# Hybrid decoder layer: accumulators cleared in a step ahead of their rows, and a norm's squares ahead of the last convolution block

## The chip, the cores and the metric

One core of a Trainium2 chip runs the whole program in one launch. The metric is the device time of that launch in microseconds (us). The kernel before took 1226.35 us, the median of three runs (1225.25 to 1227.09).

## What is computed

One layer of a decoder over 256 tokens with a model width of 2048, in float32. The reference, cut to its frame:

```python
c_act = jax.nn.silu(c)
mod = (c_act @ w_mod[l] + b_mod[l])[:, None, :]             # w_mod: 2048 x 12288
sh_m, sc_m, g_m, sh_f, sc_f, g_f = jnp.split(mod, 6, axis=-1)
h = rmsnorm(x, mix_pre_w[l]) * (1 + sc_m) + sh_m
y = hybrid_mixer(h, ...)      # h @ w_in, short gated convolution | gated linear attention, then @ w_out
x = x + g_m * rmsnorm(y, mix_post_w[l])
h = rmsnorm(x, ffn_pre_w[l]) * (1 + sc_f) + sh_f
y = conv_ffn(h, ...)          # h @ w_up, causal convolution, silu gate, @ w_down
x = x + g_f * rmsnorm(y, ffn_post_w[l])
```

Inside the mixer the attention's output goes through a norm of its own, per head: `o = rmsnorm(o, gla_norm_w) * silu(r)`, and the two halves (convolution, attention) are concatenated ahead of `w_out`. The six vectors of `mod` are matrix-vector products: each is a sum of 2048 rows of `w_mod`, scaled by `c_act`.

## The kernel before

**Units.** Every large product is cut into units. A unit has one weight tile `raw`, loaded by SP; ScalarE (ACT) casts it to a short high part `wh` (L140), VectorE (DVE) forms the rest, `wl = raw - wh` (L145), and TensorE (PE) multiplies high by high, high by low and low by high. The ring of `raw` tiles has six places, those of `wh` and `wl` three each. I number the units in program order: u0 to u57 are the product with `w_in` (its last chunk of five row blocks is u40 to u57), u58 to u73 the product with `w_out`, u74 and on those with `w_up` and then `w_down`. The code's list `tail` begins at u40, so `tail[j]` is u(40+j). L579 to L581 are the three products of a `w_in` unit, L846 to L848 those of a `w_out` unit, L990 and L992 those of `w_up`.

**Order.** `drive` (L74) writes the program unit by unit: for unit i it runs the list `early`, then the load of unit i+2 and its cast (`prep`), then `wl` of unit i+1 (`low`), then `pre`, the products of unit i, `mid`, the evacuations that are due, and `late`. Everything that is not a unit's own work hangs in these four lists. Each engine runs its instructions strictly in the order that this writes; there is no scheduler behind it. So a DVE instruction that waits holds up every later one on DVE, the next `wl` among them, and PE waits for that `wl`.

**Modulation rows.** `mod_steps` (L160) computes a part of `mod` on DVE. One step loads a block of `w_mod` (SP, L184 or L187) and adds it, scaled by one column of `c_act`, to an accumulator (L136, a scalar_tensor_tensor). Sixteen steps, "rows" from here on, make a set. The accumulator is a tile `macc` of two buffers (or, for the small first set, a tile `big`); step 0 has POOL clear it (L178) and load the bias `b_mod` into its row 0 (L179), and then does the first row. `spread` (L68) puts the steps of a set evenly into the lists `early` and `mid` of a range of units. The sets in order are those of the chunks 1 to 3 of `w_in` (u0 to u9, u12 to u21, u22 to u31, with `lag` 1: a row is added one step behind its load), then `gacc` (`g_m`, u32 to u47), f1 (`sh_f` and `sc_f`, first half, u48 to u67 without u55 to u57), f2 and the last one in the `w_up` units; those four have `lag` 0.

**Other work in u40 to u57.** The levels of the attention (L704, L740, L761 on DVE, scores by PE at L678), its output and its norm: `norms` in the list `late` of u55 has ACT take eight sums of squares (L387) and one square root (L792), `scaled` in `pre` of u56 has DVE take the reciprocal (L797) and ACT scale eight blocks (L802), which PE then transposes (L810). The convolution runs in four pairs (`CONV`): `first` (c0) multiplies two blocks on DVE (L605, `cc = cc * cx`) and scales them on ACT (L607); c1 and c2 follow a unit later (L136 with `conv` scalars, L614, L616, L620). Partial sums of `cc`, `cx` and `v` in the last chunk are added to what stands in SBUF by an accumulating DMA: ACT copies the sum out of PSUM to `hf` (L459), POOL issues the DMA (L460).

Of the kernel before, what the change touches and what calls it, by code (L numbers as in the profile page):

```python
# [6 lines left out]
F32 = mybir.dt.float32  # L7
# [7 lines left out]
P = 128  # L15
D = 2048
T = 256
KT = D // P
# [23 lines left out]
MODS = (10, 22, 32, 48, 68)  # L42
CHUNK1 = 12
# [21 lines left out]
        self.hold = 0  # L65


def spread(steps, units):  # L68

    places = [p for u in units for p in (u.early, u.mid)]  # L70
    for i, f in enumerate(steps):
        places[i * len(places) // len(steps)].append(f)

# [30 lines left out]
def layer_kernel(ctx: ExitStack, tc, x, c, w_mod, b_mod, mix_pre_w, mix_post_w, w_in, conv_w, gate_w2, gate_b,  # L104
                 gla_norm_w, w_out, ffn_pre_w, ffn_post_w, w_up, ffn_conv_w, w_down, ident_in, masks_in, out):
    nc = tc.nc
# [6 lines left out]
    wts = ctx.enter_context(tc.tile_pool(name="wts", bufs=2))  # L113
# [5 lines left out]
    def nm(s):  # L119
        uid[0] += 1  # L120
        return f"{s}_{uid[0]}"

    def slot(shape, dt=F32):
        return big.tile(shape, dt, tag="big", name=nm("big"))
# [7 lines left out]
    def raw_tile(shape):  # L132
        return wts.tile(shape, F32, tag="raw", name=nm("raw"), bufs=NRAW)

    def stt(o, a, s, b, op0=ALU.mult, op1=ALU.add):
        nc.vector.scalar_tensor_tensor(o, a, s, b, op0=op0, op1=op1)  # L136
# [22 lines left out]
    b_mod_v = b_mod.rearrange("l (s n) -> l s n", s=6)  # L159

    def mod_steps(s0, n, a, w, nj, lag=0):

        accs, cur, rows = [], {}, []

        def use(j, r):
            stt(cur["acc"], r, c_act[:, j:j + 1], cur["acc"])

        def step(j):  # L170
            if j >= KT:
                use(*rows.pop(0))
                return
            if j == 0:
                acc = cur["acc"] = (slot([P, n, w]) if n * w <= 1024 else
                                    wts.tile([P, n, w], F32, tag="macc", name=nm("macc"), bufs=2))
                accs.extend(acc[:, s, :] for s in range(n))
                nc.gpsimd.memset(acc, 0.0)  # L178
                nc.gpsimd.dma_start(acc[0:1, :, :], b_mod_v[:, s0:s0 + n, a:a + w])  # L179
            m = nj if j < KT - nj or nj < 4 else 2  # L180
            if j % m == 0:
                cur["r"] = raw_tile([P, m, n, w])
                if m == 1:
                    nc.sync.dma_start(cur["r"][:, 0, :, :], w_mod_v[:, j, s0:s0 + n, a:a + w])  # L184
                else:
                    for s in range(n):
                        nc.sync.dma_start(cur["r"][:, :, s, :], w_mod_v[:, j:j + m, s0 + s, a:a + w])  # L187
            rows.append((j, cur["r"][:, j % m, :, :]))
            if j >= lag:
                use(*rows.pop(0))  # L190

        return accs, [lambda j=j: step(j) for j in range(KT + lag)]

    W0 = CHUNKS[0] * P
    first_acc = slot([P, 2, W0])
# [104 lines left out]
    def mod_columns(accs, n, pre, tagname):  # L300

        ash = const.tile([P, 2 * n], F32, tag=tagname, name=nm("ash"))
        st = {}

        def products(tiles=None):
            r = ones if len(accs) == 2 else ones_r
            if "ps" not in st:
                st["ps"] = bank([P, 4 * n + P])  # L310
            for o in (range(2 * n) if tiles is None else tiles):
                cs = slice((o % n) * P, (o % n + 1) * P)
                terms = (accs[o // n],) if len(accs) == 2 else accs[2 + o // n]
                for j, t in enumerate(terms):
                    nc.tensor.matmul(st["ps"][:, 2 * o:2 * o + P], t[:, cs], r, start=j == 0, stop=j == len(terms) - 1)  # L315

        def columns():
            nc.vector.tensor_copy(ash[:, :n], st["ps"][:, 0:2 * n:2])
            stt(ash[:, n:], st["ps"][:, 2 * n:4 * n:2], 1.0, pre, ALU.add, ALU.mult)

        return ash, products, columns

    def mod_rows(accs, post, tiles):

        parts = []

        def load():
            parts.extend(tiles())
            for h, g in enumerate(parts):
                nc.gpsimd.dma_start(g, post[:, h * 1024:(h + 1) * 1024].rearrange("a n -> (a n)")  # L330
                                    .partition_broadcast(P))

        sums = {}

        def products(h):
            terms, r = (accs[1], ones_r) if len(accs) == 2 else ((accs[0],), ones)
            for q in range(2):
                cs = slice(h * 1024 + q * 512, h * 1024 + (q + 1) * 512)
                ps = sums[h, q] = bank([P, 512])
                for j, term in enumerate(terms):  # L340
                    nc.tensor.matmul(ps, r, term[:, cs], start=j == 0, stop=j == len(terms) - 1)

        def used(h):
            for q in range(2):
                s = slice(q * 512, (q + 1) * 512)
                nc.vector.tensor_mul(parts[h][:, s], sums[h, q], parts[h][:, s])
            gpw[h] = parts[h]

        return load, products, used
# [114 lines left out]
    def modulate_chunk(ci, ash, early=None):  # L464

        k0, k1 = bounds[ci], bounds[ci + 1]
        kept = []

        def at_once():

            n = CHUNKS[0]
            for kts in pairs(k0, k1):
                ps, hf = early.pop(0), hf0[:, kts[0]:kts[-1] + 1, :]
                d = hts[kts[0] // 2] = slot([P, 2, 2, T], F32R)
                ab = [(ash[:, n + k:n + k + 1], ash[:, k:k + 1]) for k in kts]
                for i, (a, b) in enumerate(ab):
                    nc.scalar.activation(d[:, i, 0, :], ps[:, i, :], AF.Identity, bias=b, scale=a)
                for i, (a, b) in enumerate(ab):
                    nc.vector.tensor_scalar(hf[:, i, :], ps[:, i, :], a, b, op0=ALU.mult, op1=ALU.add)
                    h32.setdefault(ci, {})[kts[i]] = hf[:, i, :]  # L480
                act_low(d, hf)
                kept.append((kts, hf, None))

        def first():
            if early:
                at_once()
                return
            for kts in pairs(k0, k1):
                ps = turn_norm(xs, kts)
                hf = hf_tile()  # L490
                modulate(ps, kts, ash, CHUNKS[ci], k0, hf)
                for i, k in enumerate(kts):
                    h32.setdefault(ci, {})[k] = hf[:, i, :]
                kept.append((kts, hf, act_high(kts, hf, hts)))

        def second():
            for kts, hf, parts in kept:
                if parts:
                    act_low(*parts)
                for i, k in enumerate(kts):  # L500
                    gate_terms.append((k, hf[:, i, :]))

        return first, second
# [599 lines left out]
    chunks = [in_units(ci) for ci in range(len(CHUNKS))]  # L1103
# [53 lines left out]
    allin = [u for c in chunks for u in c] + owait  # L1157
# [3 lines left out]
    at, seconds = 0, []  # L1161
    for ci in range(1, len(CHUNKS)):
        n, us = CHUNKS[ci], chunks[ci - 1]
        st = {}
        st["accs"], steps = mod_steps(0, 2, bounds[ci] * P, n * P, 2 if n <= 4 else 1, 1)
        spread(steps, allin[CHUNK1 if ci == 2 else at:MODS[ci - 1]])
        at = MODS[ci - 1]

        def cols(ci=ci, n=n, st=st):
            st["ash"], products, st["columns"] = mod_columns(st["accs"], n, pre_c[:, bounds[ci]:bounds[ci + 1]], f"ash{ci}")  # L1170
            products()

        def mod0(ci=ci, st=st):
            st["columns"]()
            st["m"] = modulate_chunk(ci, st["ash"])
            st["m"][0]()

        us[-LEAD].early.append(cols)
        us[-LEAD].late.append(mod0)
        seconds.append((us[-LEAD + 1].late, lambda st=st: st["m"][1]()))  # L1180
        seconds.append((us[-LEAD + 1].late if ci > 1 else chunks[1][GATE1].mid, gate_products))
        seconds.append((chunks[ci][0 if ci > 1 else GATE1 + 1].mid, gate_sum))

    tail = chunks[-1] + owait
    gacc, gsteps = mod_steps(2, 1, 0, 2048, 1)
    spread(gsteps, [u for i, u in enumerate(allin) if at <= i < MODS[3]])
    load, ones_rows, rows_used = mod_rows(gacc, mix_post_w, lambda: [slot([P, 1024]) for _ in range(2)])
    r0 = 2
    owait[r0].late.append(load)
# [44 lines left out]
        tail[GATE[e] - 1].late.append(lambda e=e: turn(e))  # L1234
    for i, u in enumerate(CONV):
        c0, c1, c2 = conv_pair(i)
        tail[u].late.insert(0, c0)
        tail[u + 1].pre.append(c1)
        tail[u + (1 if i < 3 else 2)].late.append(c2)
    owait[8].late.append(warm_sqrt)  # L1240
# [238 lines left out]
```

## Time and profile before

| | before |
|---|---|
| median of three runs | 1226.35 us (1225.25 to 1227.09) |
| the profiled execution | 1225.3 us |
| its span, from the first to the last instruction | 1223.5 us |
| granted TensorE clock, mean | 0.992 |
| PE, DVE, ACT, POOL busy | 97%, 77%, 47%, 4% of the span |
| instructions | 17251 |

The profile is of one execution, so a time in it is to be set against 1225.3 us and not against the median. A row of the timeline has the start in us from the first instruction, the duration, the engine, the line, the operation with its output and inputs, a count of like instructions in one row (`x8`), and in brackets how long the engine sat idle before it and what released it. "PEclk" is the TensorE clock that was granted, as a share of full speed; PE's busy time also counts products at a reduced clock. DMA share is the mean busy share of the 16 DMA engines. A matmul's row overlaps the next, so the pitch of products is read from a count in a window and not from a duration. DMA is seen twice: at its issue (SPq, POOLq) and by the time from issue to landing.

### The profile page before, as it was taken

The page shows a single profiled execution, that of the slowest core. Times are in us where ns is not written, and L with a number is a line of the kernel's source. Part 1 is how long each engine was busy: PE and PEld are TensorE (multiplying, and loading weights), DVE is VectorE, ACT ScalarE, POOL GpSimd, SP SyncE. Part 2 cuts the span into 40 slices and gives each one's busy share as a digit, 9 for nine tenths or more (in the row PEclk, how much of TensorE's full clock was granted, in tenths as well). Part 3 has the DMA queues.
Part 4 walks back from the last instruction along what each step waited for, and adds up shares of the span by engine and source line. Part 5 has one row for each costly group of instructions (what it writes and reads, how often), then busy time and mean ns, then how long its engine had stood idle before and what let it go on. Part 6 is the DMA issues. An engine that isn't in the chain of part 4 may idle for free.

```text
span 1223.5 us, 17251 instructions
## 1 busy us (share of the span) xinstructions
PE 1181.0 (97%) x7051; PEld 1043.6 (85%) x7051; DVE 939.0 (77%) x950; ACT 578.0 (47%) x666; POOL 44.7 (4%) x64
## 2 busy tenths in 40 slices
PE   3899999998989999999999999999999999999997
PEld 3899999998878788888888888888888888888885
DVE  6989899898979887984698979698885665444463
ACT  3663333363565437434464454454545543434452
POOL 3000100001100001000000000000000000000000
PEclk9999999999999999999999999999999999999998
DMA  9999999998879995996766767767674665555522
GB/s 342 386 359 390 319 373 396 330 292 285 245 264 334 391 379 216 347 342 218 246 213 236 251 235 240 261 204 267 233 231 150 243 246 197 199 181 205 189 87 69
DMA packets 128350, 323.87 MB, mean 265 GB/s; under 512 B 8501, under 2 KB 34437, under 8 KB 118544
## 3 DMA queue, kind: packets, MB, share of 16 engines
q1 hardware_dynamic: 124048, 312.63, 71.9%
q0 software_dynamic: 4080, 10.15, 3.1%
q8 instruction: 55, 0.90, 0.3%
q14 instruction: 23, 0.19, 0.0%
q10 hardware_dynamic: 144, 0.01, 0.0%
HBM read 315.42 MB, written 4.19 MB: 261 GB/s over the span
## 4 chain that ended last, share of the span: by engine, by line
PE 85%; DMA 4%; issue 4%; DVE 4%; ACT 1%; POOL 0%; SPq 0%; DVEq 0%; ACTq 0%; POOLq 0%
PE ps L990 27%; PE ps L992 14%; PE ps L848 9%; PE ps L847 9%; PE ps L846 9%; PE ps L581 5%; PE ps L579 5%; PE ps L580 5%; DMA raw<-in_w_mod_dram 2%; DMA big<-hf 1%; DVE macc L136 1%; DVE wl L145 1%; PE ps L315 1%; DMA big<-in_w_mod_dram 1%; DVE big L136 1%
## 5 line engine op out<-in xcount | busy, mean ns | idle before, releaser
L140 ACT CAST wh<-raw 128x2048 fp32r<-128x2048 f32 (+3 forms) x199 | 366.0, 1841 | 499.9 <-PE ps L990 192.1
L145 DVE TENSOR_TENSOR wl<-raw,wh 128x2048 fp32r<-128x2048 f32 (+3 forms) x199 | 437.3, 2200 | 144.4 <-ACT wh L140 144.4
L990 PE MATMUL ps<-big,wh 128*128 128x512 f32 x1400 | 495.0, 399 | 0.0
L992 PE MATMUL ps<-big,wl 128*128 128x256 f32 x1400 | 392.9, 281 | 0.0
L990 PEld LDWEIGHTS ps<-big,wh 128*128 128x128 f32 x1400 | 263.1, 188 | 65.0
L992 PEld LDWEIGHTS ps<-big,wl 128*128 128x128 f32 x1400 | 264.4, 189 | 0.0
L581 PE MATMUL ps<-big,wl 128*128 128x256 f32 x760 | 216.6, 285 | 4.2 <-DVE wl L145 4.2
L579 PE MATMUL ps<-big,wh 128*128 128x256 f32 x760 | 218.0, 287 | 0.0
L580 PE MATMUL ps<-big,wh 128*128 128x256 f32 x760 | 216.0, 284 | 0.0
L136 DVE SCALAR_TENSOR_TENSOR macc<-raw,c_act,macc 128x2048 f32<-128x2048 f32 (+1 forms) x96 | 199.4, 2077 | 6.2 <-issue 4.3
L846 PE MATMUL ps<-wh,big 128*128 128x512 f32 x456 | 179.4, 393 | 0.0
L847 PE MATMUL ps<-wl,big 128*128 128x512 f32 x456 | 178.4, 391 | 0.3 <-DVE wl L145 0.3
L848 PE MATMUL ps<-wh,big 128*128 128x512 f32 x456 | 178.2, 391 | 0.0
L581 PEld LDWEIGHTS ps<-big,wl 128*128 128x128 f32 x760 | 146.7, 193 | 5.5 <-DVE wl L145 5.5
L579 PEld LDWEIGHTS ps<-big,wh 128*128 128x128 f32 x760 | 146.8, 193 | 1.6 <-issue 1.3
L580 PEld LDWEIGHTS ps<-big,wh 128*128 128x128 f32 x760 | 146.9, 193 | 0.2
L847 PEld LDWEIGHTS ps<-wl,big 128*128 128x128 f32 x456 | 86.2, 189 | 18.9 <-DVE wl L145 0.9
L848 PEld LDWEIGHTS ps<-wh,big 128*128 128x128 f32 x456 | 86.1, 189 | 18.0
L846 PEld LDWEIGHTS ps<-wh,big 128*128 128x128 f32 x456 | 86.2, 189 | 17.7 <-issue 0.2
L136 DVE SCALAR_TENSOR_TENSOR big<-big,fcw,big 128x254 f32<-128x254 f32 (+1 forms) x176 | 72.1, 475 | 0.0
L916 DVE TENSOR_TENSOR big<-big,ps 128x256 f32<-128x256 f32 x88 | 31.1, 414 | 49.2 <-ACT big L914 49.2
L936 ACT ACTIVATE big<-big,fcw 128x256 f32<-128x256 f32 x88 | 37.9, 515 | 11.5 <-DVE big L927 11.5
(213 smaller groups left out, 673.1 us busy)
## 6 DMA issues: line engine op xcount, KB each, us to landing
raw<-in_w_up_dram SPq DMA_DIRECT2D x88, 1024.0 KB, 5.3
raw<-in_w_mod_dram SPq DMA_DIRECT2D x64, 1024.0 KB, 7.3
raw<-in_w_down_dram SPq DMA_DIRECT2D x44, 1024.0 KB, 4.8
raw<-in_w_in_dram SPq DMA_DIRECT2D x28, 960.0 KB, 8.4
raw<-in_w_mod_dram SPq DMA_DIRECT2D x32, 640.0 KB, 7.3
raw<-in_w_out_dram SPq DMA_DIRECT2D x16, 1024.0 KB, 7.8
raw<-in_w_in_dram SPq DMA_DIRECT2D x12, 1024.0 KB, 8.9
raw<-in_w_mod_dram SPq DMA_DIRECT2D x22, 512.0 KB, 8.4
```

The costliest lines, as they stand in the source:

```text
L136: nc.vector.scalar_tensor_tensor(o, a, s, b, op0=op0, op1=op1)
L140: nc.scalar.copy(hi, raw)
L145: nc.vector.tensor_sub(lo, raw, hi.bitcast(F32))
L579: nc.tensor.matmul(ps, w[0][:, kk, cs], ht[:, k % 2, 0, :], start=st, stop=False)
L580: nc.tensor.matmul(ps, w[0][:, kk, cs], ht[:, k % 2, 1, :], start=False, stop=False)
L581: nc.tensor.matmul(ps, w[1][:, kk, cs], ht[:, k % 2, 0, :], start=False, stop=sp)
L846: nc.tensor.matmul(ps, a[:, i, 0, ts_], w[0][:, kk, ns], start=st, stop=False)
L847: nc.tensor.matmul(ps, a[:, i, 0, ts_], w[1][:, kk, ns], start=False, stop=False)
L848: nc.tensor.matmul(ps, a[:, i, 1, ts_], w[0][:, kk, ns], start=False, stop=sp)
L936: nc.scalar.activation(st["c"][:, o, :], st["u"][o], AF.Copy, scale=fcw[:, 2, ch + o:ch + o + 1])
L990: nc.tensor.matmul(pss[o], wh[:, kk, cs], h2[k // 2][:, k % 2, :, :], start=(first and kk == 0), stop=False)
L992: nc.tensor.matmul(pss[o][:, 1, :], wl[:, kk, cs], h2[k // 2][:, k % 2, 0, :], start=False, stop=(last and kk == 3))
```

## The change

It has three parts. The clearing of an accumulator and the load of its bias leave step 0 and become a step of their own, `begin`, ahead of the sixteen rows, so that `spread` has one step more to place: 17, or 18 with a lag of 1. For the sets up to u47, `spread` may also use the list `late` of each chunk's last unit. And a convolution pair's c0 is appended to its unit's `late` where it was put in front before.

```diff
-def spread(steps, units):
-
-    places = [p for u in units for p in (u.early, u.mid)]
+def spread(steps, units, last=()):
+
+    places = [p for u in units for p in ((u.early, u.mid, u.late) if u in last else (u.early, u.mid))]
...
+        def begin():
+            acc = cur["acc"] = (slot([P, n, w]) if n * w <= 1024 else
+                                wts.tile([P, n, w], F32, tag="macc", name=nm("macc"), bufs=2))
+            accs.extend(acc[:, s, :] for s in range(n))
+            nc.gpsimd.memset(acc, 0.0)
+            nc.gpsimd.dma_start(acc[0:1, :, :], b_mod_v[:, s0:s0 + n, a:a + w])
+
         def step(j):
             if j >= KT:
                 use(*rows.pop(0))
                 return
-            if j == 0:
-                acc = cur["acc"] = (slot([P, n, w]) if n * w <= 1024 else
-                                    wts.tile([P, n, w], F32, tag="macc", name=nm("macc"), bufs=2))
-                accs.extend(acc[:, s, :] for s in range(n))
-                nc.gpsimd.memset(acc, 0.0)
-                nc.gpsimd.dma_start(acc[0:1, :, :], b_mod_v[:, s0:s0 + n, a:a + w])
...
-        return accs, [lambda j=j: step(j) for j in range(KT + lag)]
+        return accs, [begin] + [lambda j=j: step(j) for j in range(KT + lag)]
...
-        spread(steps, allin[CHUNK1 if ci == 2 else at:MODS[ci - 1]])
+        spread(steps, allin[CHUNK1 if ci == 2 else at:MODS[ci - 1]], [c[-1] for c in chunks])
...
-    spread(gsteps, [u for i, u in enumerate(allin) if at <= i < MODS[3]])
+    spread(gsteps, [u for i, u in enumerate(allin) if at <= i < MODS[3]], [c[-1] for c in chunks])
...
-        tail[u].late.insert(0, c0)
+        tail[u].late.append(c0)
```

The `lag` of each set stays what it was, and no instruction is added or removed. PE's and POOL's instructions keep their order; DVE, ACT and SP run the same ones in another.

The first place is on DVE where f1 begins (`macc_3023` is f1's accumulator, `wl_3045` before and `wl_3042` after the low part of u49's weights, the next `wl` that of u50). Before:

```order
L761 COPY_PREDICATED big_2750<-masks,ps_2942 128x512
L704 TENSOR_TENSOR big_2564<-big_2562 128x1024
L136 SCALAR_TENSOR_TENSOR macc_3023<-raw_3026,c_act,macc_3023 128x2048
L145 TENSOR_TENSOR wl_3045<-raw_2949,wh_2951 128x1920
L740 TENSOR_TENSOR big_2564<-big_2564,big_904 128x64x8
L740 TENSOR_TENSOR big_2564<-big_2564,big_838 128x64x8
L761 COPY_PREDICATED big_2750<-masks,ps_3029 128x512
L761 COPY_PREDICATED big_2750<-masks,ps_3034 128x512
L704 TENSOR_TENSOR big_2563<-big_2562 128x1024
L136 SCALAR_TENSOR_TENSOR macc_3023<-raw_3115,c_act,macc_3023 128x2048
L145 TENSOR_TENSOR wl_3134<-raw_3041,wh_3043 128x1920
```

And of the changed kernel, whose line numbers are one higher there:

```order
L762 COPY_PREDICATED big_2750<-masks,ps_2942 128x512
L705 TENSOR_TENSOR big_2564<-big_2562 128x1024
L145 TENSOR_TENSOR wl_3042<-raw_2949,wh_2951 128x1920
L741 TENSOR_TENSOR big_2564<-big_2564,big_901 128x64x8
L741 TENSOR_TENSOR big_2564<-big_2564,big_835 128x64x8
L762 COPY_PREDICATED big_2750<-masks,ps_3026 128x512
L762 COPY_PREDICATED big_2750<-masks,ps_3031 128x512
L705 TENSOR_TENSOR big_2563<-big_2562 128x1024
L136 SCALAR_TENSOR_TENSOR macc_3023<-raw_3112,c_act,macc_3023 128x2048
L145 TENSOR_TENSOR wl_3131<-raw_3038,wh_3040 128x1920
```

f1's first row has moved from ahead of u49's `wl` to ahead of u50's, and every later one up to u54 by a unit likewise: seven rows stand in u48 to u54 before, six after.

The second place is on ACT at the end of u55 (`junk` rows are the norm's squares, `big_496` the last convolution pair's block, `wh_3633` and `wh_3630` the cast of u58's weights). Before:

```order
L140 CAST wh_3558<-raw_3556 128x1280
L607 ACTIVATE big_496<-big_420,sv 128x256 x2
L387 ACTIVATE junk_3613,gss<-ps_3540 128x256
L387 ACTIVATE junk_3615,gss<-ps_3540 128x256
L387 ACTIVATE junk_3617,gss<-ps_3543 128x256
L387 ACTIVATE junk_3619,gss<-ps_3543 128x256
L387 ACTIVATE junk_3621,gss<-ps_3546 128x256
L387 ACTIVATE junk_3623,gss<-ps_3546 128x256
L387 ACTIVATE junk_3625,gss<-ps_3551 128x256
L387 ACTIVATE junk_3627,gss<-ps_3551 128x256
L792 ACT_TABLE_LOAD
L792 ACTIVATE grs<-gss,eps_t 128x8
```

After, on ACT at the same place:

```order
L388 ACTIVATE junk_3607,gss<-ps_3537 128x256
L388 ACTIVATE junk_3609,gss<-ps_3537 128x256
L388 ACTIVATE junk_3611,gss<-ps_3540 128x256
L388 ACTIVATE junk_3613,gss<-ps_3540 128x256
L388 ACTIVATE junk_3615,gss<-ps_3543 128x256
L388 ACTIVATE junk_3617,gss<-ps_3543 128x256
L388 ACTIVATE junk_3619,gss<-ps_3548 128x256
L388 ACTIVATE junk_3621,gss<-ps_3548 128x256
L793 ACT_TABLE_LOAD
L793 ACTIVATE grs<-gss,eps_t 128x8
L608 ACTIVATE big_496<-big_416,sv 128x256 x2
L140 CAST wh_3630<-raw_3628 128x2048
```

The pair's scaling (L607 before, L608 after) has moved from ahead of the squares to behind the square root; u58's cast follows in both.

The third place is on DVE at the beginning of `w_out`, from u59's `wl` (`wl_3755`, `wl_3752`) to u60's (`wl_3800` in both). Before:

```order
L136 SCALAR_TENSOR_TENSOR macc_3023<-raw_3748,c_act,macc_3023 128x2048
L145 TENSOR_TENSOR wl_3755<-raw_3702,wh_3704 128x2048
L462 TENSOR_TENSOR big_536<-big_536,ps_3708 128x512
L136 SCALAR_TENSOR_TENSOR big_576<-ps_3742,sv,big_576 128x256 x2
L145 TENSOR_TENSOR wl_3800<-raw_3751,wh_3753 128x2048
```

After, on DVE:

```order
L136 SCALAR_TENSOR_TENSOR macc_3023<-raw_3745,c_act,macc_3023 128x2048
L145 TENSOR_TENSOR wl_3752<-raw_3699,wh_3701 128x2048
L463 TENSOR_TENSOR big_536<-big_536,ps_3705 128x512
L136 SCALAR_TENSOR_TENSOR big_576<-ps_3739,sv,big_576 128x256 x2
L136 SCALAR_TENSOR_TENSOR macc_3023<-raw_3793,c_act,macc_3023 128x2048
L145 TENSOR_TENSOR wl_3800<-raw_3748,wh_3750 128x2048
```

Between the `wl` of u59 and that of u60 stands one row more than before; from u60's `wl` on, both kernels have done eight rows of f1.

## The prediction

> **What bounds the kernel now.** I begin with the page's first part and then the windows, to see whose work sets the time and where.
>
> ```profile
> span 1223.5 us, 17251 instructions
> PE 1181.0 (97%) x7051; PEld 1043.6 (85%) x7051; DVE 939.0 (77%) x950; ACT 578.0 (47%) x666; POOL 44.7 (4%) x64
> ```
>
> The windows' columns are: stretch, its length, then busy time of PE, weight loads, DVE, ACT and POOL, PE's granted clock, DMA share, GB/s.
>
> ```profile
> 20.00:60.00 40.00, 35.75 (x260) 32.67 (x259) 36.31 (x38) 23.74 (x34) 0.00 (x0) 1.00 1.05 386
> 60.00:286.00 226.00, 226.00 (x1850) 220.32 (x1850) 206.75 (x165) 97.37 (x88) 13.52 (x13) 1.00 0.98 351
> 286.00:372.00 86.00, 74.90 (x540) 71.43 (x539) 71.20 (x79) 47.84 (x88) 8.27 (x11) 0.92 0.79 251
> 372.00:400.00 28.00, 28.00 (x125) 22.09 (x124) 28.00 (x24) 13.13 (x11) 0.84 (x1) 1.00 0.99 360
> 470.00:1215.00 745.00, 744.91 (x3944) 637.57 (x3944) 525.88 (x570) 355.66 (x387) 8.19 (x12) 1.00 0.64 223
> ```
>
> PE is the bound: from 60 to 286 and from 470 to 1215 it has no gap. A reordering that leaves PE's order alone, as this one does, can gain only where PE loses time: in 20 to 60 (4.2 us idle), and in 286 to 372. There it is idle for 86.00 − 74.90 = 11.1 us and runs at a mean clock of 0.92, which by 86 × 0.08 is another 6.9: about 18.0 us in all. Next, what PE waits for (producer, total, times, longest):
>
> ```profile
> PE ps L239 <- DMA sv_r<-in_gla_norm_w_dram: 10.8, 1, 10.8
> PE ps L400 <- DVE big L1117: 7.6, 1, 7.6
> PE ps L810 <- ACT big L802: 4.2, 2, 3.6
> PE ps L581 <- DVE wl L145: 4.2, 6, 0.9
> PE ps L678 <- DVE big L740: 3.9, 2, 3.1
> PE ps L678 <- ACT hf L459: 2.2, 1, 2.2
> ```
>
> The first two lie in the start, which the change doesn't reach. L581's are those of 20 to 60. The others lie in 286 to 372; each is followed back below.
>
> **First part: the clear ahead of the rows.** The first set's sums end like this:
>
> ```profile
> 57.56 2.61 DVE L136 SCALAR_TENSOR_TENSOR big<-raw,c_act,big 128x1024 f32<-128x1024 f32 x2
> 60.43 2.02 PE L315 MATMUL ps<-ones,big 128*128 128x128 f32 x16
> ```
>
> In 20 to 60 the DMA share is 1.05: the loads are the bound, the last rows start when theirs land, and PE's column sums (L315) follow. The change leaves the bytes ahead of them as they are, so L315 stays at 60.4 and the 4.2 us of idling ahead of it only move: 0, at most 0.4 us. The sets of u12 to u47 lie under the gapless PE: 0, as long as no `wl` comes late.
>
> Where f1 begins it is otherwise:
>
> ```profile
> 283.91 0.85 POOL L460 DMA_DIRECT2D big<-hf  x1 [7.01 <-ACT hf L459]
> 284.44 2.13 POOL L178 MEMSET macc<- 128x2048 f32 x1
> macc<-in_b_mod_dram POOLq DMA_DIRECT2D x1, 8.0 KB, 5.5
> 286.87 1.23 DVE L704 TENSOR_TENSOR big<-big 128x1024 f32<-128x1024 f32 x1
> 292.42 2.35 DVE L136 SCALAR_TENSOR_TENSOR macc<-raw,c_act,macc 128x2048 f32<-128x2048 f32 x1 [4.32 <-issue]
> 294.69 2.15 DVE L145 TENSOR_TENSOR wl<-raw,wh 128x1920 fp32r<-128x1920 f32 x1
> 298.19 1.06 PE L678 MATMUL ps<-big 128*128 128x128 f32 x7 [3.07 <-DVE big L740]
> ```
>
> The trace puts the row's 4.32 us to "issue", but the cause stands beside it: POOL clears `macc` only after an accumulating DMA that it had to wait 7.01 us to issue, and the bias lands 5.5 us after its own issue, when the clear is over, at 286.57 at the earliest: 292.1. Behind the row on DVE stand u49's `wl` and L740, for which PE then waits 3.07 us. After, POOL's order is the same and the clear as late, but the row stands a unit further back: DVE goes on with `wl` at 288.1. So 4.32 of waiting and one row go, and a row costs the pitch to the next start, 294.69 − 292.42 = 2.27. DVE is **6.6 us** earlier through the rest of `w_in`.
>
> The row now due first must not wait in its turn. The row that stands ahead of u50's `wl` was at 300.31 and comes to 293.7; the bias lands at 292.3 (its 292.42 row started right then). And its load:
>
> ```profile
> 284.56 0.37 SPq L184 DMA_DIRECT2D raw<-in_w_mod_dram  x1
> raw<-in_w_mod_dram SPq DMA_DIRECT2D x64, 1024.0 KB, 7.3
> 300.31 2.34 DVE L136 SCALAR_TENSOR_TENSOR macc<-raw,c_act,macc 128x2048 f32<-128x2048 f32 x1
> ```
>
> The issue at 284.56 is of f1's third row; even such a one lands by 291.9, and the first is issued two rows earlier.
>
> **Second part: the norm's squares ahead of the last convolution pair.** The end of u55:
>
> ```profile
> 348.50 1.26 ACT L140 CAST wh<-raw 128x1280 fp32r<-128x1280 f32 x1
> 348.90 0.86 POOL L460 DMA_DIRECT2D big<-hf  x1 [7.16 <-ACT hf L459]
> big<-hf POOLq DMA_DIRECT2D x1, 256.0 KB, 5.2
> 354.17 0.69 DVE L605 TENSOR_TENSOR big<-big,big 128x512 f32<-128x512 f32 x1 [2.66 <-DMA big<-hf]
> 354.90 0.91 ACT L607 ACTIVATE big<-big,sv 128x256 f32<-128x256 f32 x2 [5.13 <-DVE big L605]
> 361.03 0.30 ACT L792 ACTIVATE grs<-gss,eps_t 128x8 f32<-128x8 f32 x1
> 361.36 0.20 DVE L797 RECIPROCAL grs<-grs 128x8 f32<-128x8 f32 x1 [5.10 <-ACT grs L792]
> 363.90 0.47 PE L810 MATMUL ps<-ident,big 128*128 128x128 f32 x1 [3.57 <-ACT big L802]
> ```
>
> ACT sits idle for 5.13 us, from 349.77, because its next instruction, L607, waits for L605, which waits for the accumulating DMA; the squares, which need neither, stand behind it. DVE in turn idles 5.10 us ahead of the reciprocal, and PE 3.57 ahead of the transposes. After, ACT goes from the cast into the squares, and in `before`'s time the reciprocal could be ready 5.13 earlier for the wait and about 0.8 for L607. But DVE, in order, still has L605's DMA ahead of it: the work there moves up to the shift of the first part (6.6) and what the norm's wait held: 5.10 of idling, of which some 0.1 stays. So DVE is a further **5.0 us** earlier, 11.6 in all, at u58's `wl`.
>
> **What comes back.** f1's row that left `w_in` is done ahead of u60's `wl`: +2.3, so DVE is 9.3 earlier from there on. That counts, since DVE has no idle time in 372 to 400 (28.00 of 28.00). PE is not as tight there:
>
> ```profile
> 403.66 2.28 DVE L145 TENSOR_TENSOR wl<-raw,wh 128x2048 fp32r<-128x2048 f32 x1
> 409.01 0.39 PE L847 MATMUL ps<-wl,big 128*128 128x512 f32 x1
> ```
>
> This is u65's `wl` and PE's first use of it: the `wl` is ready at 403.66 + 2.28 = 405.94, PE comes 3.07 later. Before it PE lost 18.0 us that it need not lose, so it can arrive 3.07 closer: 9.3 + 3.07 = 12.4. Of the `w_out` units this one leaves PE least room; from u66 on PE itself holds up the casts and DVE falls behind no more. A cross-check: the three waits of DVE that go are 4.32, 2.66 and 5.10, together 12.1 of the 14.8 us that DVE idles in 286 to 372, and DVE's work up to u65's `wl` is the same in both.
>
> **The sum** against 1225.3 us of the profiled execution (span 1223.5 and 1.8 around it): −6.6 − 5.0 + 2.3 − 3.1 = −12.4, 1212.9. The median lies 1.05 above that execution: **1214.0 us**.
>
> The sum needs no term for the clock, as long as PE waits for DVE. What the trace shows of it:
>
> ```profile
> 320.00:327.00 7.00, 7.00 (x50) 7.00 (x50) 6.97 (x9) 6.56 (x16) 2.21 (x3) 0.79 1.02 237
> 368.00:370.00 2.00, 2.00 (x6) 1.54 (x6) 2.00 (x2) 1.97 (x3) 0.00 (x0) 0.50 0.88 311
> ```
>
> After the 2.2 us wait of L678 the clock falls (0.79 in 320 to 327), after the 3.57 us wait too (0.50 in 368 to 370). I expect pauses under 2 us in their place and leave 0 for the clock; if the first stretch stays slow, that is 7.0 × 0.21 = 1.5 us of PE's, the end of the range for it. [...]
>
> **The rivals.**
>
> *The DMA decides, gain 4.8 to 7.5.* In 372 to 400 the DMA share is 0.99. One row's load of 1 MB more falls into the `w_out` units, at 360 GB/s some 2.9 us. And L605 hangs on the accumulating DMA still. All twelve of these took (min, median, max):
>
> ```profile
> DMA to landing us min/median/max: 3.3/7.4/10.3
> ```
>
> The one that matters took 5.2; now that it is issued earlier, beside more loads, it could take 10.3, and L605 with what follows on DVE comes 5.1 later. One alone gives 1214.0 + 5.1 = 1219.1, both about 1222. For it: the shares 0.99 and 1.05. Against: 251 GB/s in 286 to 372. [...]
>
> *More comes off, gain up to 18.* If `w_out` proves to have more room than u65's row says (PE's whole loss goes), 1225.3 − 18.0 + 1.05 = 1208.4. Against it: DVE's full window.
>
> *The change doesn't do what it says.* Rows one place behind their loads would need a lag; that of f1 stays 0, so a row can wait for its load as it did for its clear. If f1's first row does (6.6 lost) and the DMA of L605 takes its longest (5.1), 0.7 is left: 1225.7, no change. Against it are the 291.9 and 293.7 above.
>
> *Slower.* With its reserve gone, PE meets every `wl` of u59 to u65 just as it is ready, and pauses in each unit. If these pauses bring the clock to half, as the 3.57 us one did, a unit's 24 products, at 28.00/125 = 0.224 us each now, take up to 5.4 us more, and `wl` no longer decides. Three such units eat the 12.4; with four it is 1214.0 + 4 × 5.4 = 1235.6. For it: half clock right after 365, at u58. Against it: DVE's round there is a row, a `wl` and two small ones (2.35 + 2.28 + about 1.3 = 5.9 us) against 5.4 of PE, a pause of 0.5 a unit, and pauses of up to 0.9 (L581's) in 20 to 60 left the clock at 1.00.
>
> **How the numbers follow.** The forecast (1211 to 1217) gets 0.62, the DMA rival 0.17, more gain 0.09, no change 0.06, slower 0.06. The 0.62 holds the unknown sizes: 1.5 for the clock, 1 to 2 us for u65's room. From 1209 to 1222 lies the forecast, the DMA rival and part of the larger gain, over 8 in 10. A measurement of this kernel tells some 0.2% (2.5 us) from no change; faster than that are the first three, 0.88.
>
> **What would show it.** Right: f1's first L136 without a wait and behind u49's `wl`; the 3.07 at L678 gone; squares right behind the cast at u55; the 3.57 at L810 under 1; clock near 1.00 in 286 to 372; L315 still at 60.4; PE short of time at u65's `wl`, and the rest gapless. Wrong: waits of L136 for `raw`; a wait of L605 for `hf` over 6 us; idle PE at L847 with a clock under 1.00; new waits of PE after 470.

## The result, and the profile after

The changed kernel takes 1213.01 us (median of five runs, 1212.11 to 1213.29) against 1226.35 before: a ratio of 0.9892 with a 95% interval of 0.9878 to 0.9907, or 13.3 us. Beside later groups of runs the kernel before stood at 1225.27 to 1225.93, and the changed kernel, measured again, at 1213.19 against 1225.34, which is 12.2 us; the span's 12.3 agrees with that. The forecast was 1214.0, out of a range of 1209 to 1222. The page of the profiled execution has the span 12.3 us shorter, and PE's busy time down by 4.8: the same 7051 products, fewer of them at a reduced clock. The page counts four instructions more than before, none of them in the engines' counts.

```profile
span 1211.2 us, 17255 instructions
PE 1176.2 (97%) x7051; PEld 1040.3 (86%) x7051; DVE 940.2 (78%) x950; ACT 577.2 (48%) x666; POOL 43.5 (4%) x64
```

The windows show where it came from. The first stretch, under the loads, has as much idle time as before within a microsecond (3.4 us against 4.2), and its end, the column sums of L316 (L315 before), starts at 60.19 against 60.43. The stretch that was lossy idles for 3.8 us where it idled for 11.1, at a clock of 0.98 where it had 0.92.

```profile
20.00:60.00 40.00, 36.65 (x263) 33.65 (x261) 36.75 (x39) 24.00 (x35) 0.00 (x0) 1.00 1.05 386
286.00:372.00 86.00, 82.24 (x599) 78.36 (x598) 80.48 (x88) 53.85 (x93) 8.01 (x11) 0.98 0.89 286
```

```profile
60.19 2.02 PE L316 MATMUL ps<-ones,big 128*128 128x128 f32 x16 [0.40 <-DVE big L136]
```

PE's waits between 286 and 372 are down to two. L811 (L810) and the scores' wait for L741 (L740) are gone.

```profile
PE ps L582 <- DVE wl L145: 2.2, 1, 2.2
PE ps L679 <- ACT hf L460: 1.5, 1, 1.5
```

Where f1 begins, the timeline has POOL as late as before, but DVE goes from L705 straight into u49's `wl`; the first row stands behind it, without a wait, after the bias has landed (286.64 + 5.2 = 291.8). That `wl` starts at 287.75 and not at 294.69: 6.9 us earlier.

```profile
284.21 2.14 POOL L174 MEMSET macc<- 128x2048 f32 x1
286.64 0.54 POOL L175 DMA_DIRECT2D macc<-in_b_mod_dram  x1 [0.30 <-POOL macc L174]
```

```profile
macc<-in_b_mod_dram POOLq DMA_DIRECT2D x1, 8.0 KB, 5.2
```

```profile
286.63 1.23 DVE L705 TENSOR_TENSOR big<-big 128x1024 f32<-128x1024 f32 x1
287.75 2.17 DVE L145 TENSOR_TENSOR wl<-raw,wh 128x1920 fp32r<-128x1920 f32 x1
...
293.39 2.38 DVE L136 SCALAR_TENSOR_TENSOR macc<-raw,c_act,macc 128x2048 f32<-128x2048 f32 x1
```

At the end of u55, ACT goes from the cast (342.50 to 343.77) into the squares. The square root is there 12.0 us earlier (348.99 against 361.03), and DVE waits 0.78 us for it where it waited 5.10.

```profile
342.50 1.27 ACT L140 CAST wh<-raw 128x1280 fp32r<-128x1280 f32 x1
343.66 0.39 ACT L388 ACTIVATE junk<-ps 128x256 bf16<-128x256 f32 x1
...
348.99 0.30 ACT L793 ACTIVATE grs<-gss,eps_t 128x8 f32<-128x8 f32 x1
349.20 0.90 ACT L608 ACTIVATE big<-big,sv 128x256 f32<-128x256 f32 x2
```

```profile
346.45 0.69 DVE L606 TENSOR_TENSOR big<-big,big 128x512 f32<-128x512 f32 x1 [0.94 <-DMA big<-hf]
347.06 1.48 DVE L145 TENSOR_TENSOR wl<-raw,wh 128x1280 fp32r<-128x1280 f32 x1
349.33 0.20 DVE L798 RECIPROCAL grs<-grs 128x8 f32<-128x8 f32 x1 [0.78 <-ACT grs L793]
```

And at u65 the room is used up: its `wl` is ready at 394.21 + 2.30 = 396.51, PE uses it at 396.57 after a wait. DVE is 9.4 us earlier than before there, PE 12.4.

```profile
394.21 2.30 DVE L145 TENSOR_TENSOR wl<-raw,wh 128x2048 fp32r<-128x2048 f32 x1
396.57 0.50 PE L848 MATMUL ps<-wl,big 128*128 128x512 f32 x1 [0.35 <-DVE wl L145]
```

### The profile page after: what moved, and what is told of

It reads as the page before. It is cut to its first block, busy times and chain, and to the rows that moved or that the text cites. A ratio compares the mean times of both kernels' runs of the same rounds, so it can differ in the third digit from the quotient of the medians.

```text
span 1211.2 us, 17255 instructions
## 1 busy us (share of the span) xinstructions
PE 1176.2 (97%) x7051; PEld 1040.3 (86%) x7051; DVE 940.2 (78%) x950; ACT 577.2 (48%) x666; POOL 43.5 (4%) x64
## 4 chain that ended last, share of the span: by engine, by line
PE 83%; DVE 6%; issue 5%; DMA 3%; ACT 1%; SPq 1%; POOL 0%; DVEq 0%; ACTq 0%; POOLq 0%
PE ps L991 27%; PE ps L993 14%; PE ps L848 8%; PE ps L849 8%; PE ps L847 8%; PE ps L580 5%; PE ps L582 5%; PE ps L581 5%; DVE big L136 2%; DMA raw<-in_w_mod_dram 1%; DVE macc L136 1%; DVE wl L145 1%; PE ps L316 1%; DMA big<-in_w_mod_dram 1%; DMA big<-hf 1%
## 5 line engine op out<-in xcount | busy, mean ns | idle before, releaser
L581 PE MATMUL ps<-big,wh 128*128 128x256 f32 x760 | 215.8, 284 | 0.0
L848 PE MATMUL ps<-wl,big 128*128 128x512 f32 x456 | 177.6, 389 | 0.3 <-DVE wl L145 0.3
L581 PEld LDWEIGHTS ps<-big,wh 128*128 128x128 f32 x760 | 146.5, 193 | 0.1
L848 PEld LDWEIGHTS ps<-wl,big 128*128 128x128 f32 x456 | 85.6, 188 | 18.5 <-DVE wl L145 0.8
```

The lines of the kernel that those rows point to most:

```text
L581: nc.tensor.matmul(ps, w[0][:, kk, cs], ht[:, k % 2, 1, :], start=False, stop=False)
L848: nc.tensor.matmul(ps, a[:, i, 0, ts_], w[1][:, kk, ns], start=False, stop=False)
```

## Experiments

The theory: DVE's order decides; what DVE gains ahead of a `w_out` unit's `wl`, together with the room that PE has there, is what the end gains. Its rivals: each removed wait of PE is worth its own idle time; the loads or the accumulating DMA decide; the other sets' moves have a part in it. The kernel before stood beside each group of runs: 1225.27 us (first four), 1225.93 (next four), 1225.34 (last four).

**Rows alone.** The changed kernel with

```diff
-        tail[u].late.append(c0)
+        tail[u].late.insert(0, c0)
```

> The changed kernel with a convolution pair's c0 put in front again, so only the clears and rows are moved. Theory (DVE's order decides, and u65's low part is the place that counts): DVE is about 6.0 us earlier at u58 (6.6 less what u54's wait for the accumulating DMA takes), 2.3 of it goes to the row that comes back, PE uses up its 3.1 us of room: 1226.35 - 6.0 + 2.3 - 3.1 = 1219.5 us (1218.5 to 1220.5). Rival (each removed wait of PE is worth its own idle time): only the 3.07 us before the scores goes, 1223.3 us. The 5.1 us of DVE ahead of the reciprocal and over 3 us of PE ahead of the transposes stay under both.

1219.3 us against 1225.27, a ratio of 0.9952 (0.9939 to 0.9964): 6.0 us where 6.9 were expected. The span fell by 5.5. DVE is 6.2 us earlier at u59's `wl` and 3.9 at u65's, as expected, but PE doesn't use u65's room up. The transposes still wait for the norm, and the clock falls behind that:

```profile
PE ps L811 <- ACT big L803: 3.0, 2, 2.3
```

```profile
358.00:366.00 8.00, 6.49 (x18) 4.80 (x18) 8.00 (x7) 7.97 (x11) 0.00 (x0) 0.58 0.42 138
366.00:370.00 4.00, 4.00 (x20) 3.28 (x20) 4.00 (x5) 2.99 (x4) 0.00 (x0) 0.98 0.94 369
```

So here PE's clock decided, for which the theory had no term: PE is 6.2 us earlier at its first use of u58's `wl` (360.50 against 366.67) and only 5.5 at u59's (369.15 against 374.61), since the half clock lasts longer behind u58: from that use to about 366.2 by the windows (0.58 in 358 to 366, 0.98 in 366 to 370), 5.7 us, against 4.0 (to 370.7) in the kernel before. The rival (1223.3) is off by 4.

**Convolution alone.** The kernel before with

```diff
-        tail[u].late.insert(0, c0)
+        tail[u].late.append(c0)
```

> The kernel before with c0 appended, so only the norm's squares are moved ahead. Theory: DVE is 5.0 us earlier from u58 on, no row comes back, PE uses up its 3.1 us of room at u65: 1226.35 - 8.1 = 1218.3 us (1217.3 to 1219.3). The two halves then add up to some 15 us and not to the 13.3 measured, because each alone may use the same 3.1 us of room. Rival (own idle time): 3.57 + 0.62 us and the half clock behind it, 1220.5 us or more, and the two halves add up to 13.3 or less. The first f1 row still waits 4.3 us.

1219.52 us, 0.9952 (0.994 to 0.9965): 5.8 us, and 6.1 of the span. A miss: 8.1 were expected, and the rival's 5.9 fits the time better. DVE is 4.5 us earlier at u59 and at u65 (5.0 expected), but PE meets its `wl` at u59 already. Ready at 366.10 + 2.28 = 368.38, it is used at 368.44, so DVE's order does decide, at another unit than I had said:

```profile
366.10 2.28 DVE L145 TENSOR_TENSOR wl<-raw,wh 128x2048 fp32r<-128x2048 f32 x1
```

```profile
368.44 0.50 PE L847 MATMUL ps<-wl,big 128*128 128x512 f32 x1
```

In the kernel before, u59 had 1.73 us of room (ready at 372.88, used at 374.61), and u58 had none (ready at 366.62, used at 366.67 after a wait):

```profile
364.33 2.29 DVE L145 TENSOR_TENSOR wl<-raw,wh 128x2048 fp32r<-128x2048 f32 x1
370.60 2.28 DVE L145 TENSOR_TENSOR wl<-raw,wh 128x2048 fp32r<-128x2048 f32 x1
```

```profile
366.67 0.80 PE L847 MATMUL ps<-wl,big 128*128 128x512 f32 x1 [0.34 <-DVE wl L145]
...
374.61 0.40 PE L847 MATMUL ps<-wl,big 128*128 128x512 f32 x1
```

The two halves come to 11.7 us together (11.6 of the span), less than the whole and not more.

**Clear early, rows in place.** The changed kernel with f1's clear in u44:

```diff
     f1, fsteps = mod_steps(3, 2, 0, 1024, 1)
+    allin[44].early.append(fsteps.pop(0))
     spread(fsteps, ...)
```

> The changed kernel with f1's clear moved on to u44, so that f1's rows stand where they stood before the change and only the wait for the clear goes. Theory: the wait of 4.3 us goes, the row of 2.3 us stays in its place and none comes back in w_out, so u65 sees about the same time; some of the row is hidden by DVE's 1.9 us wait for the accumulating DMA ahead of u54's low part: 1212 us (1211 to 1213.5), no slower than the changed kernel. Rival (the row had to leave the stretch of w_in to gain): 2.3 us slower than the changed kernel, 1215.3 us.

1215.05 us, 0.992 (0.9906 to 0.9933), 2 us above the changed kernel's 1213.01; the span is 1212.4, so 1.2 longer. The theory missed, and the rival's time was near: the row had to leave. f1's rows wait no more, DVE is 9.5 us earlier at u59 and at u65, at u65 just as in the changed kernel. But at u59 the changed kernel's DVE is 11.7 earlier, since its row comes back only behind that, and here u59 is where PE stops: ready at 363.39, used at 363.44.

```profile
361.10 2.29 DVE L145 TENSOR_TENSOR wl<-raw,wh 128x2048 fp32r<-128x2048 f32 x1
```

```profile
363.44 0.50 PE L848 MATMUL ps<-wl,big 128*128 128x512 f32 x1
```

**f1 as before, all else changed.**

```diff
+    clear = fsteps.pop(0)
+    first_row = fsteps[0]
+    fsteps[0] = lambda: (clear(), first_row())
     spread(fsteps, ...)
```

> The changed kernel with f1's clear and first row in one step again, all other sets as changed. Theory: the other sets lie under a gapless PE or under the loads and are worth nothing, so this is the time of the kernel with c0 alone moved, 1218.3 us, within 0.7. Rival (the other sets' move is part of the gain): over 1 us below that run.

1219.45 us, 0.9951 (0.9938 to 0.9963), within 0.1 of the kernel with c0 alone moved, on the same chip. The other sets' moves are worth nothing that shows.

With u59 as a second place, which was taken in after these runs, the spans fall in line. Room before is 1.73 us at u59 and 3.07 at u65; the gain is the smaller of the two sums. DVE's gains are differences of the starts of the `wl` (370.60 and 403.66 before).

| kernel | DVE at u59, with room | DVE at u65, with room | smaller | span gained |
|---|---|---|---|---|
| changed | 11.70, 13.4 | 9.45, 12.5 | 12.5 | 12.3 |
| convolution alone | 4.50, 6.2 | 4.49, 7.6 | 6.2 | 6.1 |
| clear early | 9.50, 11.2 | 9.50, 12.6 | 11.2 | 11.1 |
| f1 as before | 4.95, 6.7 | 4.94, 8.0 | 6.7 | 6.5 |
| rows alone | 6.18, 7.9 | 3.92, 7.0 | 7.0 | 5.5 (half clock) |

The table leaves u58 out, and there the rule alone fails: with a room of 0.05, u58 would let the convolution alone gain 4.5 us, and it gained 6.1. The rest is clock. From its first use of u58's `wl` to that of u59's, PE takes 7.94 us in the kernel before, at half clock up to 370.7; it takes 6.26 in the convolution alone, at a clock of 1.00 in 358 to 370, and in the clear early, where no row of L848 from 357.2 to 371.5 is longer than 0.50 us (0.79 at half clock, in the rows alone); 5.91 in the changed kernel, at 1.00 from 336 to 400; and 8.65 in the rows alone, at half clock again. So 4.5 + 1.7 = 6.2 for the convolution alone, and 6.2 − 0.7 = 5.5 for the rows alone, where u58 is the place. The room of 1.73 us at u59 was itself clock that PE lost behind u58.

**A dose ahead of u65, and behind it.** To see whether u65's `wl` really decides, two DVE operations scaled by a column of zeros were added ahead of it, and in a second kernel one unit later. Both add work that the reference doesn't have.

```diff
+    zero = col(1, "zero")
+    nc.vector.memset(zero, 0.0)
+    allin[64].early.append(lambda: stt(f1[0], f1[1], zero, f1[0]) or stt(f1[1], f1[0], zero, f1[1]))
```

> The changed kernel with two extra DVE operations of 128 x 1024 (scaled by a column of zeros, some 2.4 us together) ahead of u65's low part. Theory (u65's low part decides when PE goes on): its use waits 0.1 us already, so all of it is paid: span 1211.2 + 2.4 = 1213.6 us. Rival (PE or the loads decide in w_out, DVE's order there is covered): under 0.5 us.

> The same two operations one unit later, behind u65's low part and ahead of u66's, where the trace shows 3.9 us of room. Theory: nothing is paid, span 1211.2 us within 0.5. Rival (DVE has no idle time from u54 to u66, so work anywhere in it is paid): 1213.6 us, as with the dose ahead of u65.

Ahead: 1215.75 us, 0.9917 (0.9902 to 0.9932), span 1214.6. Behind: 1211.39 us, 0.988 (0.9864 to 0.9897), span 1211.6. On one chip, the same work costs 4.4 us more a unit earlier by the medians (3.0 by the spans of the profiled executions: in the first, L316 starts 1.0 us earlier, at 58.59 against 59.60). That is more than the dose's 2.5 us (393.18 to the next start at 395.70), since the clock falls behind the pause that it makes (0.75, 0.50 and 0.90 in the three windows of 2 us from 398 to 404), and by 2 × (0.25 + 0.50 + 0.10) that is some 1.7 us of PE's work:

```profile
393.18 2.60 DVE L136 SCALAR_TENSOR_TENSOR macc<-macc,zero 128x1024 f32<-128x1024 f32 x2
395.70 2.28 DVE L145 TENSOR_TENSOR wl<-raw,wh 128x2048 fp32r<-128x2048 f32 x1
```

```profile
398.04 0.50 PE L848 MATMUL ps<-wl,big 128*128 128x512 f32 x1 [3.04 <-DVE wl L145]
```

```profile
394.00:398.00 4.00, 0.99 (x5) 0.49 (x3) 3.96 (x4) 0.00 (x0) 0.00 (x0) 1.00 1.03 425
398.00:400.00 2.00, 1.97 (x7) 1.53 (x8) 2.00 (x1) 0.00 (x0) 0.00 (x0) 0.75 1.03 422
400.00:402.00 2.00, 2.00 (x6) 1.63 (x5) 2.00 (x2) 0.00 (x0) 0.00 (x0) 0.50 1.03 422
402.00:404.00 2.00, 2.00 (x9) 1.61 (x9) 2.00 (x2) 0.00 (x0) 0.00 (x0) 0.90 1.02 418
```

With the dose behind u65, PE's waits from 372 to 420 are one of 0.4 us; without it they are one of 0.3. u65 is the place in the changed kernel, and the rival that any work of DVE in this stretch is paid falls.

**The second pair's c0 behind u54's `wl`.**

```diff
-        tail[u].late.append(c0)
+        (tail[u + 1].pre if i == 1 else tail[u].late).append(c0)
```

> The changed kernel with the second convolution pair's c0 put behind u54's low part, where before it DVE waited 1.9 us ahead of that low part for the accumulating DMA. Theory (DVE's waits for that DMA are what is left): the wait goes, DVE is 1.9 us earlier, PE's pause of 2.25 us ahead of u54's low part goes to under 0.5, and the end moves by 1.9: span 1209.3 us (1208.8 to 1210.2). Rival (the wait only moves behind, or PE's own pause at 310 decides): no change, 1211.2 us.

1211.9 us, 0.9886 (0.9871 to 0.9901); span 1209.9, so 1.3 us of the 1.9 expected. That is inside the range. The pause ahead of u54 is gone, but one of 0.7 us has come up a unit later, and not all of the 1.9 reaches the end.

**f1 spread to u70.**

```diff
-MODS = (10, 22, 32, 48, 68)
+MODS = (10, 22, 32, 48, 71)
-F2_AT = (68, 73, 16)
+F2_AT = (71, 73, 16)
```

> The changed kernel with f1's rows spread over u48 to u70 and f2's begun at u71, so that DVE does one row less ahead of u59's low part and two less ahead of u65's. Theory: DVE is 2.3 us earlier at u59 and up to 4.5 at u65, but u54's low part still hangs on the accumulating DMA, so PE is freed only of what it loses behind it (1.6 of half clock and 2.2 between 380 and 400): 1 to 2.2 us, span 1209.0 to 1210.2 us. Rival (f2's denser rows ahead of u75, where there is 1.1 us of room, give it back): 1211.2 us or more.

1209.28 us, 0.9863 (0.9849 to 0.9878); span 1207.1, 4.1 us less than the changed kernel's (1211.2 and 1211.1, from other groups of runs). More than expected, for a reason that I had wrong: u54's `wl` doesn't hang on the accumulating DMA in this kernel. A row now stands ahead of L606 and none between it and the `wl`, and L606 comes at 325.88 without a wait (326.13 after a wait of 1.91 in the changed kernel; the DMA took 7.0 us to landing here, 9.8 there). The `wl` starts 2.5 us earlier, at 326.48 against 329.00, PE doesn't pause there, and the clock stays at 1.00:

```profile
325.88 0.69 DVE L606 TENSOR_TENSOR big<-big,big 128x512 f32<-128x512 f32 x1
326.48 1.49 DVE L145 TENSOR_TENSOR wl<-raw,wh 128x1280 fp32r<-128x1280 f32 x1
```

```profile
286.00:372.00 86.00, 84.47 (x620) 80.19 (x620) 82.00 (x91) 54.87 (x95) 9.35 (x12) 1.00 0.89 292
```

The denser rows of f2 gave nothing back: PE's waits show none for them.

**What is left.** The last four ran on one chip, another than that of f1 to u70 alone: the changed kernel again, f1 to u70 with the second pair's c0 moved as above, f1 to u70 with the first pair's cast put behind the copies out of PSUM, and all three. The edit of the cast:

```diff
             nc.vector.tensor_mul(cb, cb, cx)
             mts[i] = slot([P, 2, 2, T], F32R)
-            nc.scalar.copy(mts[i][:, :, 0, :], cb)
+            if i:
+                nc.scalar.copy(mts[i][:, :, 0, :], cb)

         def third():
             cb = proj["cb" + str(i // 2)][:, s, :]
+            if not i:
+                nc.scalar.copy(mts[i][:, :, 0, :], cb)
```

> The changed kernel itself once more, beside the three variants of f1 spread to u70, so that all four stand on one chip: 1213 us within 1, span 1211.2 within 1.5 (the first 60 us under the loads differ by up to 1.9 us from profile to profile).

> f1 spread to u70, and the second convolution pair's c0 behind u54's low part too. With f1 spread, DVE waits only 1.0 us for that DMA and PE no longer pauses at u54. Theory (PE is now short of work for DVE almost nowhere; what is left is its 1.5 us pause at 310): no change from f1 spread alone, span 1207.1 us within 0.6. Rival (DVE's waits still decide): 1.0 us less, 1206.1 us.

> f1 spread to u70, and the first convolution pair's cast (ACT, which waited 4.7 us for DVE ahead of the copies out of PSUM) put behind those copies. Theory: PE's pause of 1.5 us at 310 falls to about 0.3, but u59 and u60 have 0.3 to 0.4 us of room for DVE's part, so that only 0.3 to 0.7 us reach the end: span 1206.4 to 1206.8 us. Rival (PE is free of DVE now): all of it, 1205.9 us.

> f1 spread to u70 with both of the other edits. Theory: DVE's 1.0 us and PE's 1.2 us come off together, about 1.0 to 1.2 us, span 1205.9 to 1206.2 us. Rival (the two edits don't help each other): the larger of the two single ones.

| kernel | us | ratio to before | span |
|---|---|---|---|
| changed, again | 1213.19 | 0.99 (0.9884 to 0.9917) | 1211.1 |
| f1 to u70, second pair's c0 | 1209.69 | 0.987 (0.9856 to 0.9885) | 1207.2 |
| f1 to u70, first pair's cast | 1207.29 | 0.9851 (0.9836 to 0.9866) | 1205.5 |
| all three | 1208.09 | 0.9857 (0.9842 to 0.9872) | 1205.9 |

With f1 spread, the second pair's c0 is worth nothing (as the theory had it). The wait of 1.0 us that the expectations count on stands at 343.19 there, ahead of the fourth pair, and not at u54, where L606 no longer waits. The cast takes the whole 1.6 us off the span, which the rival had, and not the 0.3 to 0.7 of the theory: DVE moved up along with PE, its `wl` at u59 from 355.56 to 354.19. Both edits together bring no more than the cast alone; the span of 1205.9 lies in the expected range, but nothing of DVE's comes off beside the cast's part, so the theory's way to it is not borne out. The best version, 1207.29 us, is 5.9 us faster than the changed kernel on the same chip; PE has no wait left in it from 286 to 450, and 85.92 of 86 us are busy:

```profile
286.00:372.00 86.00, 85.92 (x625) 81.13 (x624) 82.73 (x92) 56.21 (x95) 9.07 (x12) 1.00 0.90 296
```

## Why the prediction was right

*Where PE loses time.* Right: the end gained 12.3 us of the span, nearly all between 286 and 409 (one of L581's waits, 0.47 us at 337.14, lies there too and not in 20 to 60, which changes no term); the first 60 us and the sets of chunks 1 to 3 and `gacc` moved nothing (shown by the kernel with f1 as before).

*The clear, 6.6 us.* Right: u49's `wl` came 6.9 earlier; the row due first didn't wait, neither for the bias nor its load.

*The norm, a further 5.0, 11.6 in all.* Right: u59's `wl` came 11.7 earlier. The split is less sure: of the first half's 6.9 us at u49, 6.2 are left at u59 when the rows alone are moved, so the norm adds 5.5 there; alone, this half gives DVE 4.5.

*The row that comes back, 2.3.* Right, 11.70 − 9.45 = 2.25. But the text called it a cost only, and its place is a gain too: it comes back behind u59. Left where it was, with the clear early, the kernel was 1.2 us longer in span.

*u65 and its room of 3.07.* Right for the changed kernel, by the dose that costs on one side of u65's `wl` and not on the other. It holds only because u59 has more left (13.4 against 12.5). In the kernels with one half alone, or with the clear early, u59 is the place. The prediction didn't look at it, and my expectations for these runs failed at that.

*No term for the clock.* The sum came out, but the premise didn't hold. That pauses under 2 us leave the clock alone was an estimate. Pauses of 1.5 and 2.25 us stayed: behind the first the clock stayed at 1.00, but the second was not under 2, and behind it the clock was halved (0.50 in 332 to 334). It cost nothing in the end, since u65 waits for DVE anyway: in the kernel with the dose behind u65 the clock stayed at 1.00 there, and PE came to u65's `wl` no earlier (396.73 against 396.57). And one gain of the clock was needed: PE is 10.9 us earlier at u58 (355.74 against 366.67), and only because the half clock behind it went is it 13.0 earlier at u59 (361.65 against 374.61), with the 12.4 of u65 in reach. Where that half clock stayed, in the rows alone, the end gained 1.5 us less than u65's row allowed.

*The rivals.* The DMA had a part. These are L606's waits for it ahead of u54's `wl`, in the kernel before and in the changed one:

```profile
332.73 0.69 DVE L605 TENSOR_TENSOR big<-big,big 128x512 f32<-128x512 f32 x1 [1.64 <-DMA big<-hf]
```

```profile
326.13 0.69 DVE L606 TENSOR_TENSOR big<-big,big 128x512 f32<-128x512 f32 x1 [1.91 <-DMA big<-hf]
```

And the landings in the changed kernel, of that pair and of the one ahead of the fourth pair, which I had priced at up to 10.3:

```profile
big<-hf POOLq DMA_DIRECT2D x2, 256.0 KB, 9.8
```

```profile
big<-hf POOLq DMA_DIRECT2D x1, 256.0 KB, 3.5
```

The wait at u54 was there before (moving it behind the `wl` brought 1.3 us of the span), and the one I feared got shorter. The row's load of 1 MB cost nothing that shows either: up to u65, f1's rows wait for no load. So the DMA didn't decide. That PE pauses in each `w_out` unit and falls to half clock didn't happen (no pause over 0.3 us from 331 to 387, the clock at 1.00 from 336 to 400). A pause in a `w_out` unit with a lower clock behind it was seen with the dose of 2.5 us: 3.04 us, then 0.50 in 400 to 402. More gain than 12.4 was to be had, by moving f1's rows behind u65, and not from this change.

## What to carry to other kernels

When an engine works in order, price a removed wait at the places where its consumer has least room, in each kernel anew: the end gains the smallest of (producer's gain plus room) over these places, so halves of a change needn't add up. This holds while the consumer keeps its pace between the places; where it ran at half clock behind a wait, the clock won back is a gain of its own (1.7 us between u58 and u59 here). A step that can wait (a clear with a bias load behind it) goes well ahead of its first use, and work that may move belongs behind the last tight place, not just anywhere later. Where the trace names "issue" as the cause, look at what else the instruction needs that ends just then (here 4.32 us, with the bias landing at about 292.1 and the row starting at 292.42).

## What the runs showed of the hardware

The length of a pause alone doesn't settle whether PE's clock is halved after it. PE pauses ahead of u54's `wl` for 2.38 us in the changed kernel run again, and for 2.37 us in the one with the dose behind u65, and in both PE has one other wait from 286 to 350, of 1.5 us. In the first, the clock is then 0.50:

```profile
330.45 0.38 PE L582 MATMUL ps<-big,wl 128*128 128x256 f32 x1 [2.38 <-DVE wl L145]
```

```profile
332.00:334.00 2.00, 2.00 (x11) 2.00 (x11) 1.26 (x2) 1.21 (x3) 0.00 (x0) 0.50 0.98 356
```

In the second it stays at 1.00:

```profile
330.05 0.39 PE L582 MATMUL ps<-big,wl 128*128 128x256 f32 x1 [2.37 <-DVE wl L145]
```

```profile
332.00:334.00 2.00, 2.00 (x17) 1.94 (x17) 1.26 (x3) 1.59 (x3) 0.21 (x1) 1.00 0.98 326
```

What tells the two apart, and what brings the full clock back, these runs don't show. In the kernel before, read in windows of 0.2 us, the clock is 0.50 three times between 286 and 400: from 299.0 to 302.4 after a pause of 3.07 us (up to 298.19), from 319.5 to 322.9 after one of 2.22 (up to 318.51), and from 363.9 to 370.7 after the one of 3.57 (up to 363.90). In the changed kernel it is 0.50 once there, from 331.5 to 334.9, after the pause of 2.25 us (up to 330.54); after the one of 1.51 us (up to 311.63) it stays at 1.00.
